# Operand tiles of the pairs' products with high and low part of each chunk side by side

## The chip, the cores and the metric

The kernel runs on one core of a Trainium2 chip. A core has TensorE (matmul; weight loads are a queue of their own, PEld in the profile), VectorE (DVE), ScalarE (ACT), GpSimd (POOL) and SyncE (SP, which here only issues DMAs). Data is worked on in SBUF, an on-chip memory of 128 partitions; products arrive in PSUM. All addresses below are bytes within one partition. The metric is the time of one execution in device microseconds, as the median of several runs.

## The reference, cut to what matters

One layer of a decoder over 512 prompt tokens and 64 sample tokens (576 columns), width 1024: a half-step SwiGLU feed-forward (FFN, inner width 2816), a mixing layer with many projections, and a second FFN. Each is preceded by a normalisation with shift and scale.

```python
def swiglu(h, w_gate, w_up, w_down):
    return (jax.nn.silu(h @ w_gate) * (h @ w_up)) @ w_down

h = modulate(rms_norm(x, n1_g), sh1, sc1)
x = x + 0.5 * g1 * swiglu(h, w1_gate, w1_up, w1_down)
h = modulate(rms_norm(x, nm_g), sh2, sc2)
mix, S_new, v_rows = token_mix(h, pos0, S0, w_in, ...)   # z = h @ w_in, split in eight
x = x + g2 * mix
h = modulate(rms_norm(x, n2_g), sh3, sc3)
x = x + 0.5 * g3 * swiglu(h, w2_gate, w2_up, w2_down)
```

All is in 32-bit floats, and the change concerns the products `h @ w_gate`, `h @ w_up` and a part of `h @ w_in`.

## The kernel before, in words

**Three matmuls for one product.** TensorE takes operands that are rounded (fp32r). To keep precision each operand is split into a high part (a rounding cast on ScalarE) and a low part (what is left, a subtract on VectorE), and a product is the sum of three matmuls: high weights by high operand, high weights by low operand, low weights by high operand.

**Pairs.** Two blocks of 128 output columns, such as one of the gate and one of the up weights, form a pair. The pair's 2 x 2 blocks (first and second half of the 1024 rows, first and second half of the 576 tokens) are multiplied by a scheme of seven products in place of eight: sums and differences of weight blocks and of token blocks are formed first. The operands of these products are made once for a stage and serve for all of its pairs. There are seven: `N11`, `N1`, `T2`, `N3`, `N4`, `B21` and `B22`. Each covers 512 rows, that is four chunks of 128 rows, and `H` = 288 tokens. Three stages use them: the first FFN, the projections of the mixing layer that stream through pairs, and the second FFN.

**The operand tiles.** `op` (lines 517 to 521) gives each operand one tile, out of a pool `xa` of four or a pool `xs1` of three such tiles. A tile has 2 x 4 x 288 numbers a partition: four chunks of the high part and then four of the low part. `Operands.hi` and `Operands.lo` (lines 561 to 575) fill it, two chunks (`2j` and `2j + 1`) at a time: a cast on ScalarE, then a subtract on VectorE. The sources (`hb`, or `x` in the middle stage) hold 576 tokens for each chunk, so a half of 288 tokens is read with a gap; the differences `tx` are read without.

**One product.** `prod` (lines 647 to 655) issues 12 matmuls for four chunks `j` in turn, in one order throughout:

```python
for j in range(4):
    for z, (s, m) in enumerate(((wh, xh), (wh, xl), (wl, xh))):
        PE.matmul(ps[:, :H], lhsT=s[:, j * P:(j + 1) * P], rhs=m[:, j, :], ...)
```

So a chunk's high part is streamed, then its low part, then its high part again, against a weight block of 128 columns (512 bytes) that is loaded anew each time. While one matmul streams, the weights of the next are loaded.

**The weight tiles.** `whl` (lines 166 to 172) gives the tiles for split weights. Most hold two blocks (`Weights.put_hi` with two names: tag `whl`, four buffers out of the pool `wp`). The block `a12` of a pair is alone (tag `whs`, one buffer of a pool of its own). `set_in` (lines 148 to 156) puts the data `at` elements into a tile that is `room` elements larger than they need, so that the place of the data within a block of addresses can be chosen: `INTO` is 28 elements, 112 bytes, for both kinds here. By the addresses that the program allots, paired weights start 240 bytes past a multiple of 256 and single ones 112 bytes past one; operand tiles start 128 bytes past one. `MID`, 45 elements, is the place for other weights (down projections and more), which other matmuls use (line 485).

**Pools.** `xa`, `xs1`, `sn` and `whs` are opened one behind another (lines 123 and 124, and for the second FFN lines 866 and 867), and the pool `raw` for incoming weights behind them. It serves as one of the landing places of weights, and for the conditioning vector's weights (`ada`), which matmuls of line 307 stream.

**Order of the work.** At the start of each of the three stages the order of all steps is written out by hand (`BEGIN`, `INTO_MIX`, `INTO_FFN2`): names such as `N11h0` and `N11l0` are the cast and the subtract of an operand's first two chunks, `h0a0`, `P1` and so on are products. Behind that, loops issue one pair after the other (`stream`, `ffn`). Weights come by SyncE's DMAs.

Of the kernel before, what the change touches and what calls it, by code (L numbers as in the profile page):

```python
# [15 lines left out]
P = 128  # L16
# [7 lines left out]
H = T // 2  # L24
# [13 lines left out]
INTO = 28  # L38
# [46 lines left out]
def layer_kernel(ctx: ExitStack, tc: tile.TileContext, a):  # L85
# [7 lines left out]
    wp = ctx.enter_context(tc.tile_pool(name="wp", bufs=1))  # L93
# [16 lines left out]
    def nm(s):  # L110
        count[0] += 1
        return f"{s}_{count[0]}"


    now = {"wraw": None, "slu": None}
# [18 lines left out]
    def nine(home, shape, dt=F32R):  # L134
        return now[home].tile(shape, dt, tag="x", name=nm(home), bufs=4 if home == "xa" else 3)
# [12 lines left out]
    def set_in(home, shape, room=INTO, at=INTO, **kw):  # L148

        n = 1  # L150
        for d in shape[1:]:
            n *= d
        t = home.tile([P, n + room], F32R, **kw)[:, at:at + n]
        if len(shape) == 4:
            return t.rearrange("p (a b c) -> p a b c", b=shape[2], c=shape[3])
        return t.rearrange("p (a b c d) -> p a b c d", b=shape[2], c=shape[3], d=shape[4])
# [9 lines left out]
    def whl(shape, at=INTO):  # L166
        small = len(shape) == 3 and shape[1] == 1
        tag = "whs" if small else "whl"
        return set_in(
            now["whs"] if small else wp, [P] + shape, INTO if small else 64, at,  # L170
            tag=tag, name=nm(tag), bufs=1 if small else 4,
        )

# [7 lines left out]
    def high_low(shape, at=INTO):  # L181
        t = whl([2] + shape, at)
        return t[:, 0], t[:, 1]
# [106 lines left out]
    for i in range(2):  # L290
        for n in range(NT):
            rows = P if n < 4 else NS
            t = first.tile([rows, 512], F32, name=nm("xt"))
# [221 lines left out]
    ops = {}  # L515

    def op(name):
        if name not in ops:
            t = nine("xs1" if name in ops["near"] else "xa", [P, 2, 4, H])
            ops[name] = t[:, 0], t[:, 1]  # L520
        return ops[name]

    class Operands:
# [20 lines left out]
        def s(self, p):  # L544
            c0, c1 = 2 * p, 2 * p + 2
            u4 = self.hb[:, c0:c1, NP:T].rearrange("p c (b l) -> p c b l", l=LS)
            s0 = self.sh * 8
            for m, op in ((self.g[:, c0:c1, 1:9], ALU.mult), (mT[:, s0 + c0:s0 + c1, 1:9], ALU.add)):
                DVE.tensor_tensor(out=u4, in0=u4, in1=m.unsqueeze(3).broadcast_to([P, 2, NB, LS]), op=op)
# [11 lines left out]
        def hi(self, name, j):  # L561
            hi, src = op(name)[0][:, 2 * j:2 * j + 2], self.src(name, j)
            if name == "N11":
                ACT.activation(out=hi, in_=src, func=AF.Copy, scale=-1.0)  # L564
            else:
                ACT.copy(out=hi, in_=src)

        def lo(self, name, j):
            (hi, lo), src = (t[:, 2 * j:2 * j + 2] for t in op(name)), self.src(name, j)
            if name == "N11":  # L570
                DVE.scalar_tensor_tensor(
                    out=lo, in0=src, scalar=-1.0, in1=hi.bitcast(F32), op0=ALU.mult, op1=ALU.subtract
                )
            else:
                DVE.tensor_tensor(out=lo, in0=src, in1=hi.bitcast(F32), op=ALU.subtract)
# [87 lines left out]
    class Weights:  # L663
        def put_hi(self, names, src, neg=False):
            hl = whl([2, len(names), 512])
            if neg:
                ACT.activation(out=hl[:, 0], in_=src, func=AF.Copy, scale=-1.0)
            else:
                ACT.copy(out=hl[:, 0], in_=src)  # L669
            self.hl[names] = hl, src, neg  # L670
# [297 lines left out]
    def home_whl(c, shape):  # L968
        return home_wd(c, shape) if c in (0, 1, 4, 5) else whl(shape[1:], MID)
# [858 lines left out]
    for pr in ([0], [1], [2], [3], [4], [5], [6, 7]):  # L1828
# [4 lines left out]
        for h in range(2):  # L1833
            for c in pr:
                ps = proj(W[c], OA, h)
                t = sa[c][:, PART[h]]
# [218 lines left out]
```

## Time and profile before

| what | number |
|---|---|
| time, median of three runs | 1657.79 us (1654.53 to 1658.67) |
| time of the profiled execution | 1656.22 us |
| its span, first to last instruction | 1654.4 us |
| instructions | 31368 |
| TensorE busy | 1624.5 us, 98% |
| weight loads busy | 1560.9 us, 94% |
| VectorE busy | 1153.0 us, 70% |
| ScalarE busy | 784.3 us, 47% |
| mean granted clock of TensorE | 0.996 |

The busy time of an engine counts when at least one of its instructions is under way. Matmuls overlap, so the mean duration of one (some 290 ns at 288 columns) is longer than the distance from one to the next. A group in the profile is a line of the kernel with an engine, an operation and the tiles that it writes and reads, such as `ps<-xa,whl`: into PSUM, streaming an operand tile of `xa`, against a paired weight tile. `whs` stands for a single weight tile. Where the profile shows idle time of an engine, it names what ended it.

### The profile page before, as it was taken

The page shows a single profiled execution, that of the slowest core. Times are in us where ns is not written, and L with a number is a line of the kernel's source. Part 1 is how long each engine was busy: PE and PEld are TensorE (multiplying, and loading weights), DVE is VectorE, ACT ScalarE, POOL GpSimd, SP SyncE. Part 2 cuts the span into 40 slices and gives each one's busy share as a digit, 9 for nine tenths or more (in the row PEclk, how much of TensorE's full clock was granted, in tenths as well). Part 3 has the DMA queues.
Part 4 walks back from the last instruction along what each step waited for, and adds up shares of the span by engine and source line. Part 5 has one row for each costly group of instructions (what it writes and reads, how often), then busy time and mean ns, then how long its engine had stood idle before and what let it go on. Part 6 is the DMA issues. An engine that isn't in the chain of part 4 may idle for free. (4 is left out here: it accounts for less than half of the span.)

```text
span 1654.4 us, 31368 instructions
## 1 busy us (share of the span) xinstructions
PE 1624.5 (98%) x12548; PEld 1560.9 (94%) x12548; DVE 1153.0 (70%) x1835; ACT 784.3 (47%) x1331; POOL 293.1 (18%) x372
## 2 busy tenths in 40 slices
PE   8999999999999999999999999999999999999997
PEld 4899999999999999999999999998999999999997
DVE  6867857676697777854788554676848868676773
ACT  5634524344564556553444454453236525343454
POOL 0000000000411111113346343454231000000002
PEclk9999999999999999999999999999999999999999
DMA  9553444332536776765367575799540233332331
GB/s 301 145 156 109 141 133 136 114 103 87 179 117 209 227 213 189 222 192 192 121 192 251 180 171 159 207 262 271 172 141 14 87 93 96 95 92 81 99 89 58
DMA packets 300213, 252.09 MB, mean 152 GB/s; under 512 B 13594, under 2 KB 260634, under 8 KB 300067
## 3 DMA queue, kind: packets, MB, share of 16 engines
q1 hardware_dynamic: 284594, 206.76, 41.5%
q0 software_dynamic: 13168, 40.97, 8.9%
q10 hardware_dynamic: 2304, 2.36, 0.4%
q8 instruction: 98, 1.61, 0.4%
q14 instruction: 49, 0.39, 0.1%
HBM read 207.01 MB, written 43.02 MB: 151 GB/s over the span
## 5 line engine op out<-in xcount | busy, mean ns | idle before, releaser
L651 PE MATMUL ps<-xa,whl 128*128 128x288 f32 x3000 | 423.6, 296 | 5.8 <-ACT xa L564 2.4
L651 PEld LDWEIGHTS ps<-xa,whl 128*128 128x128 f32 x3000 | 404.5, 190 | 18.5 <-issue 4.2
L651 PE MATMUL ps<-xs,whl 128*128 128x288 f32 x2040 | 289.1, 295 | 0.9 <-ACT sn L660 0.5
L651 PEld LDWEIGHTS ps<-xs,whl 128*128 128x128 f32 x2040 | 274.0, 189 | 11.0 <-issue 4.2
L679 DVE TENSOR_TENSOR whl<-wraw,whl 128x1024 fp32r<-128x1024 f32 x192 | 234.4, 1223 | 55.0 <-ACT whl L669 46.7
L669 ACT CAST whl<-wraw 128x1024 fp32r<-128x1024 f32 x192 | 200.0, 1047 | 107.9 <-DVE wraw L793 65.9
L485 PEld LDWEIGHTS ps<-c,wd 128*128 128x128 f32 x1824 | 236.9, 188 | 3.5 <-issue 3.4
L485 PE MATMUL ps<-c,wd 128*128 128x320 f32 (+1 forms) x1824 | 240.0, 292 | 0.0
L485 PE MATMUL ps<-c,whl 128*128 128x256 f32 (+1 forms) x1368 | 186.9, 294 | 1.1 <-ACT c L195 0.7
L485 PEld LDWEIGHTS ps<-c,whl 128*128 128x128 f32 x1368 | 179.4, 188 | 3.4 <-ACT c L195 1.1
L472 POOL TENSOR_TENSOR x<-x,s 128x64 f32<-128x64 f32 x72 | 36.8, 511 | 797.4 <-DVE s L471 771.6
L466 DVE SCALAR_TENSOR_TENSOR x<-ps,gate,x 128x320 f32<-128x320 f32 (+1 forms) x128 | 61.1, 481 | 111.2 <-PE ps L485 111.1
L660 ACT COPY sn<-ps 128x288 f32<-128x288 f32 x195 | 77.4, 399 | 107.2 <-PE ps L651 106.9
L188 DVE TENSOR_TENSOR whl<-wraw,whl 128x1024 fp32r<-128x1024 f32 x56 | 76.3, 1364 | 66.2 <-ACT whl L187 65.4
L952 ACT CAST wd<-wraw 128x640 fp32r<-128x640 f32 (+2 forms) x58 | 45.4, 783 | 102.3 <-PE ps L485 93.4
L1353 PE MATMUL ps<-whl,xx 128*128 128x256 f32 x768 | 88.9, 276 | 0.0
L1353 PEld LDWEIGHTS ps<-whl,xx 128*128 128x128 f32 x768 | 88.0, 188 | 0.0
L651 PE MATMUL ps<-xs,whs 128*128 128x288 f32 x480 | 69.9, 294 | 0.0
L187 ACT CAST whl<-wraw 128x1024 fp32r<-128x1024 f32 x56 | 58.6, 1049 | 21.5 <-PE ps L485 13.3
L651 PEld LDWEIGHTS ps<-xs,whs 128*128 128x128 f32 x480 | 65.7, 189 | 0.0
L669 ACT CAST whs<-wraw 128x512 fp32r<-128x512 f32 x62 | 38.5, 620 | 56.5 <-PE ps L651 46.7
L957 DVE TENSOR_TENSOR wd<-wraw,wd 128x640 fp32r<-128x640 f32 (+2 forms) x58 | 53.5, 922 | 10.3 <-ACT wd L952 10.2
(285 smaller groups left out, 2220.6 us busy)
## 6 DMA issues: line engine op xcount, KB each, us to landing
ada<-in_w_ada_dram SPq DMA_DIRECT2D x56, 512.0 KB
wraw<-in_w_in_dram SPq DMA_DIRECT2D x96, 256.0 KB
wraw<-in_w_gate_dram SPq DMA_DIRECT2D x88, 256.0 KB
wraw<-in_w_up_dram SPq DMA_DIRECT2D x88, 256.0 KB
wraw<-in_w_in_dram SPq DMA_DIRECT2D x32, 512.0 KB
wraw<-in_w_down_dram SPq DMA_DIRECT2D x32, 384.0 KB
wraw<-in_w_down_dram SPq DMA_DIRECT2D x32, 320.0 KB
accd<-c POOLq DMA_DIRECT2D x32, 288.0 KB, 5.7
```

What stands on the lines that cost most here:

```text
L187: ACT.copy(out=hi, in_=raw)
L188: now["lo"] = (eng or DVE).tensor_tensor(out=lo, in0=raw, in1=hi.bitcast(F32), op=ALU.subtract)
L466: DVE.scalar_tensor_tensor(out=x[:, o:o + w], in0=ps[:, :w], scalar=g[:, c, 0:1], in1=x[:, o:o + w], op0=ALU.mult, op1=ALU.add)
L472: return lambda: POOL.tensor_tensor(out=x[:, NP:T], in0=x[:, NP:T], in1=u, op=ALU.add)
L485: PE.matmul(ps[:, :PW[h]], lhsT=s[:, k, c0:c0 + P], rhs=m[:, PART[h]], start=k == 0 and z == 0, stop=k == kc - 1 and z == 2,)
L651: PE.matmul(ps[:, :H], lhsT=s[:, j * P:(j + 1) * P], rhs=m[:, j, :], start=fresh and j == 0 and z == 0, stop=j == 3 and z == 2, skip_group ...
L660: ACT.copy(out=t, in_=ps[:, :H])
L669: ACT.copy(out=hl[:, 0], in_=src)
L679: now["lo"] = DVE.tensor_tensor(out=hl[:, 1], in0=src, in1=hl[:, 0].bitcast(F32), op=ALU.subtract)
L952: ACT.copy(out=hl[:, 0], in_=self.raw[c])
L957: DVE.tensor_tensor(out=lo, in0=self.raw[c], in1=hi.bitcast(F32), op=ALU.subtract)
L1353: PE.matmul(ps[:, :DV], lhsT=s, rhs=m, start=i == 0, stop=i == 23)
```

## The change

`op` gives the tile as four chunks, and in each the high and the low part: `[P, 4, 2, H]` in place of `[P, 2, 4, H]`. What `op` returns has the same shape as before (four chunks of 288 for the high part, four for the low one), but consecutive chunks of a part are now 2304 bytes apart in place of 1152, and a chunk's low part lies 1152 bytes behind its high part in place of 4608. The tile's size, the pools, the instructions and their order are the same. The casts and subtracts that fill two chunks write two runs of 288 with a gap in between.

`whl` places single weights 32 elements (128 bytes) further into their tile, and gives their tile 64 elements of room, as paired ones have, in place of 28. `at` is `INTO` for the single weights here, so they start 60 elements in. Their tile is 36 elements longer.

```diff
@@ whl
         small = len(shape) == 3 and shape[1] == 1
         tag = "whs" if small else "whl"
         return set_in(
-            now["whs"] if small else wp, [P] + shape, INTO if small else 64, at,
+            now["whs"] if small else wp, [P] + shape, 64, at + 32 if small else at,
             tag=tag, name=nm(tag), bufs=1 if small else 4,
         )
@@ op
         if name not in ops:
-            t = nine("xs1" if name in ops["near"] else "xa", [P, 2, 4, H])
-            ops[name] = t[:, 0], t[:, 1]
+            t = nine("xs1" if name in ops["near"] else "xa", [P, 4, 2, H])
+            ops[name] = t[:, :, 0], t[:, :, 1]
         return ops[name]
```

## The prediction

> **What bounds the kernel now.** First the head of the page, for who is busy. The columns of its first table are busy time, share of the span and number of instructions.
>
> ```profile
> span 1654.4 us, 31368 instructions
> PE 1624.5 (98%) x12548; PEld 1560.9 (94%) x12548; DVE 1153.0 (70%) x1835; ACT 784.3 (47%) x1331; POOL 293.1 (18%) x372
> PEclk9999999999999999999999999999999999999999
> ```
>
> TensorE is busy for 98% of the span at the full granted clock, and the other engines have room. So the end is set by how closely one matmul follows another. Next comes the view of groups by line with shapes kept apart: how many matmuls stream the operand tiles (xa, xs) of the pairs' products, and against which weights (count | busy us, mean ns of one | idle before).
>
> ```profile
> L651 PE MATMUL ps<-xa,whl 128*128 128x288 f32 x3000 | 423.6, 296 | 5.8 <-ACT xa L564 2.4 <-ACT whl L669 1.4 <-DVE whl L679 1.3
> L651 PE MATMUL ps<-xs,whl 128*128 128x288 f32 x2040 | 289.1, 295 | 0.9 <-ACT sn L660 0.5
> L651 PE MATMUL ps<-xs,whs 128*128 128x288 f32 x480 | 69.9, 294 | 0.0
> L651 PE MATMUL ps<-xa,whs 128*128 128x288 f32 x264 | 38.8, 295 | 0.0
> ```
>
> These are 3000 + 2040 + 480 + 264 = 5784 matmuls of 288 columns, 12 to a product, with 6.7 us of waiting before them in all. Their pitch is read from the timeline of TensorE (start us, us, what).
>
> ```profile
> 1358.00 4.89 PE L651 MATMUL ps<-xa,whl 128*128 128x288 f32 x36
> 1362.72 1.74 PE L651 MATMUL ps<-xs,whl 128*128 128x288 f32 x12
> 1364.30 1.74 PE L651 MATMUL ps<-xa,whl 128*128 128x288 f32 x12
> 1365.87 1.74 PE L651 MATMUL ps<-xs,whl 128*128 128x288 f32 x12
> 1367.45 1.74 PE L651 MATMUL ps<-xs,whs 128*128 128x288 f32 x12
> 1369.03 4.89 PE L651 MATMUL ps<-xa,whl 128*128 128x288 f32 x36
> ```
>
> One pair's seven products, 84 matmuls, take 1369.03 - 1358.00 = 11.03 us, so 131.3 ns each. 5784 of them are 759 us, 46% of the span. A nanosecond on each is 5.8 us. A single matmul lasts longer (about 293 ns) because its end overlaps its followers; I take it that one that lasts 3 ns longer pushes the next one back by 3 ns.
>
> Now the view of one line, narrowed to moments at which exactly three matmuls are under way: those of one chunk j, streaming high, low and high part. Columns are the shortest, median and longest duration in ns. The first two rows are chunks 2 and 3 of a product against paired weights, the last two chunks 2 and 3 of one against a single weight.
>
> ```profile
> L651 PE MATMUL ps<-xa,whl x3: 289/293/293, 102.1 to 102.4; 128*128 128x288 f32 x3
> L651 PE MATMUL ps<-xa,whl x3: 293/296/296, 102.5 to 102.8; 128*128 128x288 f32 x3
> ...
> L651 PE MATMUL ps<-xs,whs x3: 294/296/296, 103.7 to 104.0; 128*128 128x288 f32 x3
> L651 PE MATMUL ps<-xs,whs x3: 289/292/296, 104.1 to 104.3; 128*128 128x288 f32 x3
> ```
>
> Same shape, same clock, but the even chunk takes (289 + 293 + 293)/3 = 291.7 ns a matmul and the odd one 295.0. With the single weight it is the other way round: even 295.3, odd 292.3. What differs is an address. A chunk is 288 x 4 = 1152 bytes, four and a half times 256, so odd chunks start half a 256-byte block beside even ones. By the program's addresses the paired weights start 240 bytes past a multiple of 256, single ones 112, so half a block apart too. **The reading on which all else rests:** moving part and weights half of 256 bytes apart in one way stand well, in the other badly.
>
> **The change, part by part.** *The tiles.* Chunk j's high part starts at 1152 j bytes in the tile and its low part 4608 bytes (18 x 256) later, so all three matmuls of a chunk are at the same place now: two chunks well placed, two badly. Afterwards the high part starts at 2304 j (9 x 256), always at the good place, and the low part 1152 bytes behind it, always at the slow one. The order is high, low, high, so two of three matmuls are at the good place, where it is one of two now. No product of the trace alternates like that, so its price is bounded from rows:
>
> - If each matmul costs the mean of its own place, the new mean is (2 x 291.7 + 295.0)/3 = 292.8 ns, against (291.7 + 295.0)/2 = 293.3 now: -0.55 ns x 5784 = -3.2 us.
> - If one badly placed stream between two well placed ones is made up for by its neighbours, each triple takes what an even chunk takes now: 291.7, -1.67 ns x 5784 = -9.6 us.
> - Outer ends: every high part at 289 and the low part at 293 (290.3, -3.0 ns, -17.4 us), and every triple as an odd chunk now (295.0, +1.67 ns, +9.6 us).
>
> I take the middle of the first two, **-6.4 us**. The even chunk's row is the nearest: it has the bad place before and after its three matmuls, and still has a 289 in it.
>
> *Single weights.* They go from 112 to 240 bytes past the multiple, like the paired ones. Without that, the 744 matmuls with single weights would have the high parts at the bad place. What the move brings by itself: the two single rows average 293.8 against 293.3, 0.5 ns x 744 = **-0.4 us**. The tile grows by 36 elements, so the pool of raw weights behind it starts some 144 bytes later. Of matmuls only those of the conditioning vector stream from there.
>
> ```profile
> L307 PE MATMUL ps<-ada,cs x224: 592/605/617, 79.0 to 735.8; 128*32 128x512 f32 x112
> ```
>
> At most the 3.3 ns between places on 224 of them, 0.7 us either way; I take nothing.
>
> *The splits.* 42 ScalarE casts and 42 VectorE subtracts that fill the tiles now write two runs of 288 elements with a gap, in place of 576 in a row. Writing with a gap is not in the trace; reading with a gap is (hb), and beside it a cast without any (g).
>
> ```profile
> L566 ACT CAST xa<-hb x10: 659/674/678, 43.7 to 1282.2; 128x576 fp32r<-128x576 f32 x10
> L692 ACT CAST c<-g x44: 666/669/676, 67.5 to 1603.9; 128x576 fp32r<-128x576 f32 x44
> ...
> L575 DVE TENSOR_TENSOR xa<-hb,xa x10: 749/752/758, 45.6 to 1283.2; 128x576 fp32r<-128x576 f32 x10
> L695 DVE TENSOR_TENSOR c<-g,c x44: 750/753/760, 68.8 to 1604.9; 128x576 fp32r<-128x576 f32 x44
> ```
>
> A gap in the source costs 5 ns on one engine and nothing on the other. 42 x 5 ns is 0.2 us, hidden behind TensorE's 98%; I take nothing. If a write with a gap were as much dearer as the whole cast, 42 x 0.67 = 28 us would be spread over ScalarE, of which only each of three stages' first operands stand before a matmul (two casts, 1.3 us a stage, 4 us); nothing speaks for that. No instruction, DMA or wait is added, and no step is moved past another on any queue. As high and low now lie interleaved, a first matmul might be held until its low part is written too: one subtract of 0.75 us in each of three stages, 2.3 us at most, of which I take none.
>
> *Does anything else become the bound?* In a stretch full of such products the engines stand so (stretch, its length, then busy time of TensorE, weight loads, VectorE, ScalarE, GpSimd; clock and DMA last):
>
> ```profile
> 1351.84:1392.83 40.99, 40.99 (x315) 40.99 (x314) 32.85 (x50) 21.29 (x35) 0.32 (x1) 1.00 0.27 80
> ```
>
> TensorE is busy throughout, VectorE 32.85 of 40.99 us, ScalarE 21.29. A matmul shorter by 1.1 ns shortens this stage by 312 x 1.1 = 0.35 us; there is room.
>
> *Sum:* -6.4 - 0.4 = -6.8 us. The profiled execution took 1656.2 us (span 1654.4 and 1.8 around it), which becomes 1649.4. The three runs' median, 1657.8, is 1.6 higher and becomes **1651.0**.
>
> **The rivals.**
>
> *A: the neighbours decide.* 289 stands once in each well placed three; it may need a well placed matmul on both sides. Then, in the new order, each high part has a low one on one side and takes 293, and a lone low part takes 293 (first of a badly placed three) or 296. The triple's mean is 293.0 to 294.0, -0.33 to +0.67 ns: -1.9 to +3.9 us, with -0.4 for the single weights 1655.5 to 1661.3. For it: where such a three starts and ends, the rows have 293, not 289. Against it: rows of the trace at such places are few and with other weights.
>
> *B, slower: each switch of place costs.* Now two of six matmuls follow one at the other place, afterwards four of six. If a switch upsets the read-ahead of the next stream, no high part comes below 293 and low parts go above 296; at the odd chunk's mean, 295.0, it is +9.6 us, 1667. It counts as slower from 0.87 ns on the mean (5 us over 5784), so from 294.2. For it: the single-weight rows, which have a switch of the weights' place close by, hold a 296 even in the well placed chunk. Against it: in the paired rows the first matmul after a switch to the bad place, 293, is the shortest of its three.
>
> *C: the place has nothing to do with it*, and even and odd differ for a reason that goes along with the order. Matmuls and weight loads would then not meet at all, and the time stays at 1657.8. The mirrored rows of the single weights, in the same order, speak against it. The Trainium skill's page "TensorE: Matmul & The Clock Gate", section "Step-by-step: what each phase is for", states this case: TensorE has two independent read ports, and "Loading the next tile's weights doesn't steal SBUF read bandwidth from the running matmul". By that rule the change is worth 0 us; the rows of this trace, 291.7 against 295.0 ns at one shape, do not agree with it.
>
> *D: the low part is made whole too*, the outer end of -17.4 us: 1640. It needs 289 twice in three, which no row has.
>
> **How the numbers follow.** Forecast, -3.6 to -10 us (1647.8 to 1654.2 by itself): 0.52, of which 0.08 is a gain of under 5 us. A 0.20, C 0.07, B 0.15, D 0.06. About 0.3%, 5 us, is what a measurement here can tell from no change. Faster: 0.44 + 0.06 = 0.50; same: 0.08 + 0.20 + 0.07 = 0.35; slower 0.15. The range of 1644 to 1663 holds the forecast, A and C and the near end of B, and leaves out D and the most of B.
>
> **What would show it.** Right: the view of three matmuls at a time gives the same three durations for even and odd chunks and for single and paired weights, with a mean near 292.2 ns; 84 matmuls of a pair take 11.03 - 84 x 0.0011 = 10.94 us; everything outside line 651 stays. Neighbours: no 289 is left. Switches: 84 matmuls take over 11.10 us. C: durations still differ by even and odd chunk. It would be wrong altogether if casts and subtracts on the tiles got longer than 0.70 and 0.80 us, or the waits before line 651 grew from 6.7 us by several.

## The result and the profile after

The changed kernel takes **1652.3 us**, median of ten runs (1651.0 to 1652.9), against 1655.9 us for ten runs of the kernel before (1654.4 to 1658.7). The ratio is 0.9976, with a 95% interval of 0.9966 to 0.9986, a gain of 2.3 to 5.6 us. The forecast was 1651.0. It stood on the median of three runs of before, 1657.8; the longer series puts before 1.9 us lower, so that 3.6 of the 6.8 us that were forecast came.

The head of the page of the changed kernel (busy time, share of the span, instructions):

```profile
span 1649.7 us, 31367 instructions
PE 1618.0 (98%) x12548; PEld 1554.7 (94%) x12548; DVE 1152.9 (70%) x1835; ACT 783.2 (47%) x1331; POOL 292.0 (18%) x372
```

The span is 4.7 us shorter, TensorE 6.5 us less busy, and the same engine bounds the kernel by the same share. The groups by line of the changed kernel, shapes kept apart (count | busy us, mean ns of one | idle before):

```profile
L651 PE MATMUL ps<-xa,whl 128*128 128x288 f32 x3000 | 420.6, 295 | 5.8 <-ACT xa L564 2.4 <-ACT whl L669 1.4 <-DVE whl L679 1.3
L651 PE MATMUL ps<-xs,whl 128*128 128x288 f32 x2040 | 287.2, 294 | 1.3 <-ACT sn L660 1.1
...
L651 PE MATMUL ps<-xs,whs 128*128 128x288 f32 x480 | 69.1, 292 | 0.0
...
L651 PE MATMUL ps<-xa,whs 128*128 128x288 f32 x264 | 38.4, 294 | 0.0
```

Their busy time is 420.6 + 287.2 + 69.1 + 38.4 = 815.3 us; before it was 423.6 + 289.1 + 69.9 + 38.8 = 821.4. The line that the change is about gives 6.1 us, spread over all four groups. The timeline of TensorE in the second FFN of the changed kernel (start us, us, what) has one pair from one row of 36 matmuls to the next:

```profile
1354.78 4.84 PE L651 MATMUL ps<-xa,whl 128*128 128x288 f32 x36
1359.46 1.72 PE L651 MATMUL ps<-xs,whl 128*128 128x288 f32 x12
...
1365.70 4.84 PE L651 MATMUL ps<-xa,whl 128*128 128x288 f32 x36
```

84 matmuls take 1365.70 - 1354.78 = **10.92 us**, 130.0 ns each; before 11.03 and 131.3.

One line narrowed to three matmuls under way (shortest, median, longest ns), an even and an odd chunk against paired weights, then the same against a single weight, in the changed kernel (the view sorts the durations; their order in time is given below):

```profile
L651 PE MATMUL ps<-xa,whl x3: 290/292/295, 102.7 to 103.0; 128*128 128x288 f32 x3
...
L651 PE MATMUL ps<-xa,whl x3: 289/293/293, 103.1 to 103.4; 128*128 128x288 f32 x3
...
L651 PE MATMUL ps<-xs,whs x3: 290/292/295, 104.3 to 104.6; 128*128 128x288 f32 x3
...
L651 PE MATMUL ps<-xs,whs x3: 289/292/293, 104.7 to 105.0; 128*128 128x288 f32 x3
```

Paired and single weights now give the same pattern, but even and odd chunks still differ in their durations. In order of time the even chunk has 290 for the high part, 292 for the low one and 295 for the second high one; the odd one 289, 293, 293. The low part at the bad place is no dearer than the second high part at the good one.

The ends of matmuls in the trace are modelled; starts are recorded. So for the experiments the distances between starts were taken too. For one product of a pair, 12 matmuls, from the records of the second FFN (ns; chunks 0 to 3, three steps each; high, low, high):

```
before  131 127 131 | 131 133 133 | 132 127 130 | 131 134 133   sum 1573
after   128 127 135 | 126 132 132 | 128 127 135 | 126 132 132   sum 1560
```

By starts, before has 389 ns for an even chunk and 397 for an odd one; the changed kernel has 390 for both. Of 433 products that are followed at once by more of the same line, 301 take 1558 to 1562 ns in the changed kernel and none of before's is below 1565 (307 take 1570 to 1578). Another 61 of the changed kernel's take 1570 to 1578, as before's do: it has a faster rhythm of 1560 ns, and it keeps to it for most products, not for all.

**Where the rest of the 6.1 us went.** One part of the profiled execution got worse: the first 41.4 us (stretch, its length, busy time of TensorE, weight loads, VectorE, ScalarE, GpSimd, then clock and DMA), the first row of before, the second of after:

```profile
0.00:41.40 41.40, 33.55 (x155) 18.61 (x156) 25.34 (x48) 23.76 (x44) 1.40 (x11) 1.00 1.02 301
```

```profile
0.00:41.40 41.40, 32.19 (x151) 17.95 (x152) 24.88 (x47) 22.94 (x44) 1.41 (x11) 1.00 0.99 292
```

TensorE does 1.4 us less work there. The view of waits names the landing of the first weights of the conditioning vector (us, times, longest), before and then after:

```profile
PE ps L307 <- DMA xs<-in_w_ada_dram: 0.4, 1, 0.4
```

```profile
PE ps L307 <- DMA xs<-in_w_ada_dram: 1.4, 2, 1.1
```

1.0 us of the 1.4 is this wait. The change does not touch these transfers, and single executions of before spread over 4.3 us, so it may be chance; with 6.1 - 1.4 = 4.7 us the span is accounted for. That ten runs show 3.6 in the median and not 4.7 lies within the interval.

The casts and subtracts that write with a gap (shortest, median, longest ns), in the changed kernel:

```profile
L566 ACT CAST xa<-hb x10: 662/673/678, 44.3 to 1279.3; 128x576 fp32r<-128x576 f32 x10
...
L575 DVE TENSOR_TENSOR xa<-hb,xa x10: 748/752/753, 46.2 to 1280.2; 128x576 fp32r<-128x576 f32 x10
```

Medians of 673 and 752 ns against 674 and 752: the gap costs nothing.

### The profile page after: what moved, and what is told of

Its sections match the earlier page's. It is cut to its first block, busy times and chain, and to the rows that moved or that the text cites. A ratio compares the mean times of both kernels' runs of the same rounds, so it can differ in the third digit from the quotient of the medians.

```text
span 1649.7 us, 31367 instructions
## 1 busy us (share of the span) xinstructions
PE 1618.0 (98%) x12548; PEld 1554.7 (94%) x12548; DVE 1152.9 (70%) x1835; ACT 783.2 (47%) x1331; POOL 292.0 (18%) x372
## 3 DMA queue, kind: packets, MB, share of 16 engines
q10 hardware_dynamic: 2304, 2.36, 0.4%
## 5 line engine op out<-in xcount | busy, mean ns | idle before, releaser
L651 PE MATMUL ps<-xa,whl 128*128 128x288 f32 x3000 | 420.6, 295 | 5.8 <-ACT xa L564 2.4
L651 PE MATMUL ps<-xs,whl 128*128 128x288 f32 x2040 | 287.2, 294 | 1.3 <-ACT sn L660 1.1
L1353 PE MATMUL ps<-whl,xx 128*128 128x256 f32 x768 | 88.9, 276 | 0.0
L651 PE MATMUL ps<-xs,whs 128*128 128x288 f32 x480 | 69.1, 292 | 0.0
L669 ACT CAST whs<-wraw 128x512 fp32r<-128x512 f32 x62 | 38.4, 620 | 55.7 <-PE ps L651 45.0
```

Source lines behind the costliest of these rows:

```text
L1353: PE.matmul(ps[:, :DV], lhsT=s, rhs=m, start=i == 0, stop=i == 23)
```

## The experiments

Four explanations were tried, in this order. *Own place*: what a matmul takes goes by whether its own stream stands well or badly against the weights, the prediction's reading. *Switches*: what costs is a change of place from one matmul to the next, rival B. *Streams that go on*: a matmul is cheap where its stream continues where the one before it ended. And, formed after the first seven runs, *the repeating order*: the places of successive matmuls form an order that repeats, and this order as a whole sets the pitch, whichever weights are used. "G" and "B" below are a stream at the good and the bad place. All experiments change the changed kernel, except where said. Each is measured by the busy time of its four groups of the pairs' line (815.3 us after, 821.4 before) and by one pair's 84 matmuls (10.92 and 11.03 us), beside the time.

**Half the clock for 3.4 us.** The busy times come from one profiled execution of each kernel, and most of these hold stretches of 3.4 us in which the granted clock of TensorE is 0.5, mostly near the beginning of a stage of pairs. Below is one of them, in the alternating kernel with its weights at 112 (described further down), and then the same window in the alternating kernel with its weights at 240, at the full clock (stretch, its length, busy time of TensorE with its matmuls, then clock and DMA):

```profile
1303.40:1306.80 3.40, 3.40 (x14) 0.50 0.59 172
```

```profile
1303.40:1306.80 3.40, 3.40 (x28) 1.00 0.43 115
```

By the records, matmuls of the pairs' line start 240 ns apart there in place of some 131, about 14 of them, so a stretch adds about 14 x 109 = 1.5 us to the four groups. Before and after have two each on this line, so their difference of 6.1 us is not touched. Other kernels have none to three (one of 6.8 us counts as two). Where it matters, the text and the tables below give their number, and the groups less 1.5 us for each, which is an estimate: 818.4 us for before and 812.3 for after. The pair in the second FFN by which kernels are compared holds none of them in any run.

### The two parts by themselves

The tiles' new order with single weights left where they were:

```diff
-            now["whs"] if small else wp, [P] + shape, 64, at + 32 if small else at,
+            now["whs"] if small else wp, [P] + shape, INTO if small else 64, at,
```

> Only the operand tiles are changed; single weights stay 112 bytes past a multiple of 256. Theory (the place of the streamed part against the weights within 256 bytes decides): the 5040 matmuls with paired weights gain as in the changed kernel, about 1.07 ns each, 5.4 us; the 744 with single weights now have their high parts badly placed, two of three, and cost some 0.5 to 2 ns more than before, 0.4 to 1.5 us. In all 3 to 4 us less than before in TensorE's pitch, so about 1652 to 1654. In the view of three matmuls, products with single weights show other durations than those with paired ones. Rival (what counts is that high and low part lie side by side, whatever the weights' place): the same durations for both kinds and the whole gain.

Measured: 1653.9 us, ratio 0.9979 (0.9971 to 0.9988). The groups by line of this kernel:

```profile
L651 PE MATMUL ps<-xa,whl 128*128 128x288 f32 x3000 | 421.6, 295 | 5.9 <-ACT xa L564 2.4 <-ACT whl L669 1.4 <-DVE whl L679 1.3
L651 PE MATMUL ps<-xs,whl 128*128 128x288 f32 x2040 | 287.4, 294 | 1.3 <-ACT sn L660 1.3
...
L651 PE MATMUL ps<-xs,whs 128*128 128x288 f32 x480 | 70.3, 295 | 0.0
...
L651 PE MATMUL ps<-xa,whs 128*128 128x288 f32 x264 | 39.0, 296 | 0.0
```

818.3 us in all. The paired groups take 3.7 us less than before, the single ones 0.6 more. The time and the single groups are as own place foresaw. By starts a product with a single weight mostly takes 1591 to 1596 ns here and the others of the pair 1558 to 1562. This execution has three half-clock stretches, so less these it is 813.8 us, against 812.3 with the whole change. By the time, the new tiles alone (0.9979) cannot be told from the whole change (0.9976).

The move of the single weights in the kernel before:

```diff
-            now["whs"] if small else wp, [P] + shape, INTO if small else 64, at,
+            now["whs"] if small else wp, [P] + shape, 64, at + 32 if small else at,
```

> Only the single weights are moved by 128 bytes; operand tiles as before. Theory (place): the durations of products with single weights become those with paired ones, 289/293/293 in even and 293/296/296 in odd chunks; the product at the change from one kind to the other loses its irregular start. Worth 0.4 to 1 us, which a measurement here can't tell from nothing. Rival (the move is a part of its own of the gain): 2 us or more.

Measured: 1655.6 us, ratio 0.9992 (0.9983 to 1.0001), 820.6 us, and 11.02 us for a pair. By itself the move cannot be told from nothing in the time, 0.8 us in the busy time. With the new tiles 818.3 - 815.3 = 3.0 us of busy time are between the kernels without and with it. Of these, 109.3 - 107.5 = 1.8 us stand in the two groups with single weights; the 1.2 us in the paired ones are about one half-clock stretch. The two parts fit together: the second keeps the first one's order the same in all seven products.

### The weights half of 256 bytes further

All weights of the products 112 bytes past a multiple of 256, so that high parts stand badly and low parts well (order B G B). The weights of the mixing layer's values, which matmuls of other lines stream, moved along:

```diff
-            now["whs"] if small else wp, [P] + shape, 64, at + 32 if small else at,
+            now["whs"] if small else wp, [P] + shape, 64, at + 32 if at == INTO and not small else at,
```

> The changed kernel with all weights of these products, paired and single, 112 bytes past a multiple of 256 in place of 240, half a block on. High parts are then badly placed and low ones well. Theory (place): two of three badly placed, so the gain is lost and more: by the mean of the places 293.9 ns against 293.3 before, 0.6 ns x 5784 = 3 us above before, about 1659; if the durations of a badly placed three (295) hold throughout, 1666. Rival (side by side is what counts, not the weights' place): as the changed kernel, 1652.

Measured: 1666.1 us, ratio 1.0055 (1.0043 to 1.0067). Two rows of its timeline and two of its groups by line:

```profile
1365.27 4.93 PE L651 MATMUL ps<-xa,whl 128*128 128x288 f32 x36
...
1376.41 4.94 PE L651 MATMUL ps<-xa,whl 128*128 128x288 f32 x36
```

```profile
L651 PE MATMUL ps<-xa,whl 128*128 128x288 f32 x3000 | 427.6, 297 | 5.8 <-ACT xa L564 2.4 <-ACT whl L669 1.4 <-DVE whl L679 1.3
...
L1353 PE MATMUL ps<-whl,xx 128*128 128x256 f32 x768 | 91.5, 279 | 0.0
```

A pair takes 11.14 us, and the four groups 828.7 us: 13.4 more than after, both with two half-clock stretches, with the same instructions in the same order, operands of the same size, and only an address moved. Line 1353, whose matmuls stream the values' weights, goes from 88.9 to 91.5 us; together with the other lines that stream them this is 4.2 us more. Of the two times that own place gave, 1659 and 1666, the upper one came, with these 4.2 us in it that were in neither. So the place matters, and much: rival C is out.

### All three matmuls of a chunk at one place

In the changed kernel's tiles, the high part is streamed in the low part's stead (the low part's product is left out), so that every stream stands well, G G G throughout:

```diff
-            for z, (s, m) in enumerate(((wh, xh), (wh, xl), (wl, xh))):
+            for z, (s, m) in enumerate(((wh, xh), (wh, xh), (wl, xh))):
```

> The changed kernel, in which the second matmul of each chunk streams the high part once more in place of the low part: the low part's product is left out of the result, the number and shape of all instructions stay. All 5784 matmuls are then at the good place. Theory (place): the middle matmul of a well placed three before took 289 ns against a mean of 293.3; if all do, 4.3 ns x 5784 = 25 us less than before, about 1631. Rival (the gain comes from the alternation of the two places from one matmul to the next): without alternation the gain is gone, 1656 or above. Rival (one address streamed over and over is dearer): above 1656.

Measured: 1659.0 us, ratio 1.0015 (1.0006 to 1.0024). From its timeline:

```profile
1359.73 4.92 PE L651 MATMUL ps<-xa,whl 128*128 128x288 f32 x36
...
1370.84 4.92 PE L651 MATMUL ps<-xa,whl 128*128 128x288 f32 x36
```

A pair takes 11.11 us, the groups 825.6: every stream at the good place, no switch at all, and slower than before. The reverse, every stream at the bad place (the low part streamed three times, the high part's products left out):

```diff
-            for z, (s, m) in enumerate(((wh, xh), (wh, xl), (wl, xh))):
+            for z, (s, m) in enumerate(((wh, xl), (wh, xl), (wl, xl))):
```

> The changed kernel, in which all three matmuls of a chunk stream the low part: the high part's products are left out of the result, the number and shape of all instructions stay. All 5784 matmuls are at the bad place and none starts where the one before it ended. Theory 1 (continuing streams): as with high parts alone, about 132.2 ns a matmul, 1659. Theory 2 (place): all badly placed, above the run with high parts alone: 133.4 ns, the pitch of a badly placed matmul after another in the kernel before, or more; 1666 and above.

Measured, in a single run: 1658.8 us, 824.8 us in the groups, 11.06 us for a pair. All well and all badly placed differ by 0.8 us of busy time. Neither own place nor switches orders these two against before and after. One reservation: both kernels read the same 1152 bytes three times running, which before and after do not, so they change more than the place.

### Every matmul at the other place than the one before it

This has no such reservation. The tile gets the old shape, and the high and the low part change places in odd chunks. A chunk's three streams are its high, low and high part again, as in the changed kernel, and the order is G B G B G B: half of the streams well placed, as before, and a switch at every step.

```diff
+    class Part:
+        def __init__(self, t, even, odd):
+            self.t, self.at = t, (even, odd)
+        def two(self, j):
+            return self.t[:, j, self.at[0]:self.at[1] + 1:self.at[1] - self.at[0]]
+        def one(self, j):
+            return self.t[:, j // 2, self.at[j % 2]]
...
-            t = nine("xs1" if name in ops["near"] else "xa", [P, 4, 2, H])
-            ops[name] = t[:, :, 0], t[:, :, 1]
+            t = nine("xs1" if name in ops["near"] else "xa", [P, 2, 4, H])
+            ops[name] = Part(t, 0, 3), Part(t, 1, 2)
...
-                    ps[:, :H], lhsT=s[:, j * P:(j + 1) * P], rhs=m[:, j, :],
+                    ps[:, :H], lhsT=s[:, j * P:(j + 1) * P], rhs=m.one(j),
```

> The changed kernel with high and low part swapped in the odd chunks of a tile (high, low, low, high, high, low, low, high). Every matmul then streams from the other place than the one before it, through whole products and from product to product. Half of the matmuls are at either place, as in the kernel before. Theory 1 (a stream that starts where the one before it ended, within 256 bytes, is cheap; one that has to jump by 128 is dear): before, two of six matmuls start so, in the changed kernel four of six, with all high parts none: 131.3, 130.3 and 132.2 ns a matmul, about 1 ns for each third. Here all six: 129.3 ns or less, 1.0 ns x 5784 = 6 us below the changed kernel, about 1646. Theory 2 (the place against the weights decides, by the share of well placed matmuls): half and half as before, 131.3 ns, 1656. Theory 3 (switches of place cost): above 1660.

Measured: 1660.9 us, ratio 1.0029 (1.0019 to 1.0040). From its timeline, where the pairs' line has number 662:

```profile
1358.24 4.93 PE L662 MATMUL ps<-xa,whl 128*128 128x288 f32 x36
...
1369.37 4.93 PE L662 MATMUL ps<-xa,whl 128*128 128x288 f32 x36
```

A pair takes 11.13 us, the groups 824.8. By own place this had to equal before (821.4); it is 3.4 us more. The profiled execution was also the fastest of eight (1657.6 us) and has no half-clock stretch, so that less these it is 824.8 against 818.4. Streams that go on do not explain it either. A stream of 1152 bytes ends half of 256 bytes beside its start, so within 256 bytes the next one begins where it ended whenever the place switches: at two of six steps in before, at four in after and in the kernel with all weights 128 bytes further, at all six here. The four have 821.4, 815.3, 828.7 and 824.8 us. Switches would fit this run alone, but not the two above.

The same with the weights 128 bytes further (the edit of the section before last beside this one, the values' weights moved along again):

> As the run with alternating places, with all weights of these products moved half a block, to 112 bytes past a multiple of 256. Theory 1: each matmul still starts where the one before it ended; good and bad places only change roles, so the time is that of the run with weights at 240, within 2 us. Theory 2 (place): half and half again, 131.3 ns, 1656. If the 14 us between the changed kernel and the one with its weights half a block on come from the weights' place as such, this run is slower than its twin by as much.

Measured: 1666.1 us, ratio 1.0060 (1.0045 to 1.0075), 829.1 us in the groups, 11.13 us for a pair. The order is the same but for its start, B G B G B G, and the second FFN's pair takes the same 11.13 us. Over all three stages the groups are 4.3 us dearer in the profile, and all of it stands in one group (the run at 240 first, then this one):

```profile
L662 PE MATMUL ps<-xa,whl 128*128 128x288 f32 x3000 | 424.2, 295 | 5.8 <-ACT xa L575 2.4 <-ACT whl L680 1.4 <-DVE whl L690 1.3
```

```profile
L662 PE MATMUL ps<-xa,whl 128*128 128x288 f32 x3000 | 428.6, 297 | 5.8 <-ACT xa L575 2.4 <-ACT whl L680 1.4 <-DVE whl L690 1.3
```

The other three groups agree within 0.1 us. This execution has three half-clock stretches, all on that group, and its twin has none: less these it is 824.6 against 824.8 us, so the two agree. Of the 5.2 us between their times, 4.2 are those of the values' lines, as above.

### The same order with other weights

The second and the third matmul of each chunk exchanged: high, high, low, so G G B. Repeated, this is the changed kernel's order G B G begun at another point, but another matmul of the three now takes the low weights.

```diff
-            for z, (s, m) in enumerate(((wh, xh), (wh, xl), (wl, xh))):
+            for z, (s, m) in enumerate(((wh, xh), (wl, xh), (wh, xl))):
```

> The changed kernel with the second and third matmul of each chunk exchanged: high weights by high part, low weights by high part, high weights by low part. Streams go high, high, low; through a product the places then repeat as before the exchange (two good ones, one bad), only shifted by one matmul, and no weight block is loaded twice in a row. Theory 4 (the repeating order of places is what sets the pitch, whichever weights are loaded): 130.3 ns a matmul as in the changed kernel, L651 in all within 1.5 us of its 772 us. Rival (loading the same weights twice in a row is part of it): over 0.5 ns a matmul apart, 3 us or more either way.

Measured, in a single run: 1651.3 us beside a single run of before at 1658.7. The groups by line:

```profile
L651 PE MATMUL ps<-xa,whl 128*128 128x288 f32 x3000 | 421.4, 295 | 5.8 <-ACT xa L564 2.4 <-DVE whl L679 1.5 <-ACT whl L669 1.4
L651 PE MATMUL ps<-xs,whl 128*128 128x288 f32 x2040 | 287.4, 294 | 1.0 <-ACT sn L660 0.7
...
L651 PE MATMUL ps<-xs,whs 128*128 128x288 f32 x480 | 69.4, 293 | 0.0
...
L651 PE MATMUL ps<-xa,whs 128*128 128x288 f32 x264 | 38.4, 293 | 0.0
```

816.6 us, within 1.3 of the changed kernel and also with two half-clock stretches, as the repeating order foresaw; also, the same stream twice running does no harm here. But it is not the same throughout. From its timeline, a row of the first FFN and two of the second:

```profile
171.77 4.84 PE L651 MATMUL ps<-xa,whl 128*128 128x288 f32 x36
...
1353.89 4.88 PE L651 MATMUL ps<-xa,whl 128*128 128x288 f32 x36
...
1364.91 4.88 PE L651 MATMUL ps<-xa,whl 128*128 128x288 f32 x36
```

36 matmuls take 4.84 us in this row of the first FFN and 4.88 in the second FFN, at one order. A pair there takes 11.02 us, 131.2 ns a matmul against 130.0 in the changed kernel, more than the 0.5 ns that the expectation allowed; in that stage it failed. By starts, 205 of 433 products take 1558 to 1562 ns and 161 take 1570 to 1578: the same order runs in one of two rhythms (in the middle stage 88 of 113 take 1560 and none 1573; in the second FFN 29 of 150 take 1560 and 105 take 1573 or 1574). The changed kernel has both too (301 and 61), and its slower one, 1573 and 1574, is also the shortest and commonest length of before.

### The place in finer steps

The changed kernel with its weights, paired and single, at four other places. Its own is 240 bytes past a multiple of 256; the number in the edit is in elements of 4 bytes, and the values' weights stay.

```diff
-    def whl(shape, at=INTO):
+    def whl(shape, at=32):
```

This one puts the weights 16 bytes further, at 256, that is 0:

> The changed kernel with the weights of these products, paired and single, at a multiple of 256 bytes (16 bytes further on); other weights stay. If what counts is which half of 256 bytes the weights lie in, the 16 bytes ahead of the multiple are a detail: within 0.3 ns a matmul (2 us) of the changed kernel. If the order of places works only through the exact time at which a load crosses from half to half, the pitch changes by 0.5 ns or more, either way.

With 12 they are 64 bytes back, at 176:

> The changed kernel with these weights 176 bytes past a multiple of 256 (64 bytes back). Between the place of the changed kernel (130.3 ns a matmul) and the one half a block off (132.6 ns): if the effect is gradual, in between, 131 to 132 ns, 4 to 9 us more in line 651. If only halves count, as one of the two ends.

With 44 (and 96 elements of room for a single weight) 64 bytes further, at 48:

> The changed kernel with these weights 48 bytes past a multiple of 256 (64 bytes on). If the effect is gradual and alike to both sides, as with 176 bytes; if there is a better place than the one that the change takes, here or at 176 the pitch falls below 130.3 ns. 48 is near the 52 bytes at which the weights of line 485 stand, whose matmuls of 320 columns take turns of 142 and 145 ns.

With 24 they are 16 bytes back, at 224:

> The changed kernel with the weights of these products 224 bytes past a multiple of 256 (16 bytes back). The places tried so far gave, in busy time of line 651: 831.6 us at 176, 815.3 at 240, 821.7 at 0, 832.9 at 48. If what is wanted is a load that begins a little ahead of the multiple, 32 bytes ahead may be as good as 16 or better: 815 us or less, 1650 to 1652. If the place must be met to 16 bytes, as 0 against 240 suggests, this loses the gain as well: 820 us or more, 1657 or above.

Measured, with the run at 112 from above; the first three new ones are single runs:

| weights start at | time, us | groups of the pairs' line, us | half-clock stretches | groups less 1.5 us each | one pair in the second FFN, us |
|---|---|---|---|---|---|
| 112 (128 back) | 1666.1 | 828.7 | 2 | 825.7 | 11.14 |
| 176 (64 back) | 1667.5 | 831.6 | 3 | 827.1 | 11.15 |
| 224 (16 back) | 1659.6 | 823.9 | 1 | 822.4 | 11.07 |
| 240 (the change) | 1652.3 | 815.3 | 2 | 812.3 | 10.92 |
| 0 (16 on) | 1656.4 | 821.7 | 1 | 820.2 | 11.01 |
| 48 (64 on) | 1664.4 | 832.9 | 2 | 829.9 | 11.20 |

At 224 the ratio to before is 1.0024 (1.0015 to 1.0033). At 48 the timeline has:

```profile
1364.29 4.97 PE L651 MATMUL ps<-xa,whl 128*128 128x288 f32 x36
...
1375.49 4.96 PE L651 MATMUL ps<-xa,whl 128*128 128x288 f32 x36
```

Of the six places tried, the new order of the tiles gains in the time at one only. The expectations of a detail (at 0) and of a gradual change (at 176 and 48) failed; that of a place which must be met to 16 bytes (at 224) came. 16 bytes to either side it is lost, and 64 bytes on it turns into 832.9 - 821.4 = 11.5 us more than before. "Well" and "badly placed" are not two broad places half of 256 bytes apart, as the prediction took them: 240 and 224 are a sixteenth of 256 apart and differ by 8.6 us, 10.1 less the stretches.

### All orders together

The weights are at 240 in the first rows and at 112 in the last two; "switches" counts, in two chunks, the matmuls that stand otherwise than the one before them.

| kernel | order of two chunks | well placed | switches | groups, us | half-clock stretches | groups less 1.5 us each |
|---|---|---|---|---|---|---|
| after | GBG GBG | 4 of 6 | 4 | 815.3 | 2 | 812.3 |
| second and third exchanged | GGB GGB | 4 of 6 | 4 | 816.6 | 2 | 813.6 |
| before | GGG BBB | 3 of 6 | 2 | 821.4 | 2 | 818.4 |
| alternating | GBG BGB | 3 of 6 | 6 | 824.8 | 0 | 824.8 |
| low part alone | BBB BBB | 0 of 6 | 0 | 824.8 | 2 | 821.8 |
| high part alone | GGG GGG | 6 of 6 | 0 | 825.6 | 2 | 822.6 |
| weights 128 further | BGB BGB | 2 of 6 | 4 | 828.7 | 2 | 825.7 |
| alternating, 128 further | BGB GBG | 3 of 6 | 6 | 829.1 | 3 | 824.6 |

Neither the share of well placed streams nor the number of switches sorts the busy times. (In before the single weights stand the other way round; the kernel with these alone moved has 820.6.) What the rows do show is that kernels with one cycle agree: the two that repeat G B G are within 1.3 us, whichever weights they use, and the two that alternate, begun at opposite places, within 0.2 less the stretches. Kernels with the same number of switches are up to 13.4 us apart, and those with the same share up to 6.4 less the stretches. That the order as a whole sets the price fits this, but it is not shown: one order can run in two rhythms, the finer places show that "G" and "B" do not describe a place fully, and each row is one execution.

## Why the prediction was right, and where its reading was not

**Bound.** Right. TensorE stayed at 98%, a shorter pitch came out as a shorter time, and the other engines did not change (VectorE 1152.9 us, ScalarE 783.2).

**The size.** About right. A pair was to take 10.94 us and takes 10.92; the mean of the two triples was to be 292.2 ns and is (292.3 + 291.7)/2 = 292.0; line 651 was to lose 6.8 us and loses 6.1. The total gained 3.6 us, less than what was called measurable (5 us): with the interval of 2.3 to 5.6 it belongs to the outcome "within 0.3%", which had 0.35, rather than to "faster", which had 0.50. The time, 1652.3, lies in the forecast's own band of 1647.8 to 1654.2; the gain is at the lower end of the band of 3.6 to 10.

**The step that failed: "moving part and weights half of 256 bytes apart in one way stand well, in the other badly".** The two rows of even and odd chunks showed that addresses matter, and that holds: one address moved costs up to 17.6 us (832.9 against 815.3). But they do not give a price of a good and of a bad place which can be carried to another order. With such prices, all streams well placed would be the best kernel; it takes 825.6 us, more than before (with the reservation made above), and the alternating kernel, which has none, would equal before; it takes 824.8 against 818.4 less the half-clock stretches. The 291.7 and 295.0 ns were the price of each chunk within before's order, and both bounds of the -6.4 us, "each matmul costs the mean of its own place" and "each triple takes what an even chunk takes now", were worked out from them. By starts the changed kernel's chunks take 390 ns each, one more than before's even chunk (389), so the second bound was nearly met, but not for its reason: it said that neighbours make up for one badly placed stream, and the opposite mixture, one well placed between two badly placed, is worse than three badly placed. That the middle of the bounds came out is in part luck.

**"The same three durations for even and odd chunks".** Not so: 290, 292, 295 and 289, 293, 293. The distances of starts do agree, 390 and 390 ns. The prediction took durations for pitch (before's even and odd chunk differ by 10 ns in the sum of three durations and by 8 in the starts); it should have read starts, which the timeline has.

**Single weights.** -0.4 us was for the move by itself; alone it measured -0.8 us of busy time and nothing clear in the time. The prediction said that without the move the 744 matmuls would have their high parts at the bad place, but gave no price. It was 109.3 - 107.5 = 1.8 us on these matmuls, with the new tiles.

**The splits and waits.** Right: 673 and 752 ns as before. Waits ahead of line 651 went from 6.7 to 7.1 us. The loss of 1.4 us at the start, by a DMA that landed later, was in no term.

**Rivals.** *A* foresaw that no 289 is left; 289 and 290 are there, ahead of a low part. *B* foresaw over 11.10 us for a pair when switches cost; with four of six switches it is 10.92, and without a switch 11.06 and 11.11. *C* is refuted by every run that moves the weights alone. The Trainium skill's page "TensorE: Matmul & The Clock Gate", section "Step-by-step: what each phase is for", says that loading the next weights takes no read bandwidth from the running matmul; here the address of the weights alone takes the same matmuls from 815.3 to 832.9 us, so the place of the weights is worth 2% here. Whether read bandwidth is what they cost the running matmul, no run shows. *D* did not come.

**What stays open.** Why an order has the pitch that it has. Matmuls and weight loads are busy at once (98% and 94% of the span), and the lengths of 12 matmuls gather at single values (such as 1560, 1573, 1580, 1590 and 1600 ns), which looks like two periodic patterns of reads that lock into each other; that is only argued. No run separates the reads of the weights from those of the stream, and the two rhythms at one order have no explanation here, nor have the stretches at half the clock. Chunks a multiple of 256 bytes apart, with gaps, so that all four stand alike, were not tried.

## What to carry to other kernels

Where matmuls follow each other without a gap and each loads new weights, the addresses of stream and weights, to 16 bytes, are a parameter worth trying: it was 2% of the matmuls' time here. Scan it on the chip, with the order of the streams, and do it anew after every change of layout. Do not work out a new order from prices per matmul of the old one. Read a pitch from the distance of starts, not from durations. And count the stretches at half the clock before busy times of two executions are compared: here three of them looked like a price of the order.

## What the runs showed of the hardware that was not expected

- Streams which all stand alike to their weights are not the cheapest: 825.6 and 824.8 us (in kernels that read one part three times running), against 815.3 for a mixture of two to one.
- 16 bytes decide: 823.9, 815.3 and 821.7 us at 224, 240 and 0 (822.4, 812.3 and 820.2 less the half-clock stretches).
- One order can run in two rhythms, about 1560 and 1573 ns for 12 matmuls, and it kept mostly to one in two of three stages of one kernel (36 matmuls in 4.84 us in a row of the first FFN and 4.88 in the second FFN).
- Matmuls of 256 columns that stream weights feel it too: 88.9 against 91.5 us on line 1353, when the stream moved by 128 bytes.
- A stretch of 3.4 us at a granted clock of 0.5 takes matmuls from 131 to 240 ns from start to start and costs about 1.5 us; the mean granted clock of before's executions ranges from 0.992 to 0.998, and two kernels that seemed 4.3 us apart agree within 0.2 us without them.
